# Attention's shift as one row, the closing norm on VectorE, and earlier work in the first stages of a one-core hybrid mixer

## The chip, the cores and the metric

The kernel runs on one NeuronCore of one Trainium2 chip. Its engines are TensorE (PE; PEld are its weight loads), VectorE (DVE), ScalarE (ACT), GpSimd (POOL) and SyncE (SP). SP issues nearly all DMA transfers. The metric is the device time of one execution in microseconds.

## The reference

x is 2048 rows of 1024 values. From a vector c come shift, scale and gate, each 1024 long, by `silu(c) @ w_ada + b_ada`. The layer then is:

```python
h = layer_norm(x) * (1 + scale) + shift
xr, zr, q, k, v, za, fl = split(h @ w_in)        # 512 wide each; fl is 8
xc = causal_conv4(xr)                             # per channel
y_r = rms_norm(rg_lru(xc)) * silu(zr)             # gated linear recurrence
d = cumsum(log_sigmoid(fl + b_fgate))             # per head
s = q @ k.T / 8 + (d[query] - d[key])             # 8 heads of 64, causal
y_a = rms_norm(softmax(s) @ v) * silu(za)
y = concat(y_r, y_a) @ w_out
out = layer_norm(2**0.25 * x + gate * y) * ln_gain + ln_bias
```

All is float32. A softmax row may be shifted by any number without changing its result.

## The kernel before

Products are made in float16 pairs: each operand is split into a high part and a low part (`split_out`, `split_T`, `split_h`), and three matmuls (high by high, high by low, low by high) add up in PSUM. Scales come from maxima over whole tensors. `all_max` takes a column of 128 partial maxima through a TensorE transpose, a VectorE maximum and a matmul with ones. Such chains are Python generators in the list `chains`; `tick` advances the first of them by one step, and `flush` runs all to their ends. A projection calls `tick` after every quarter or eighth of its matmuls.

The order of the program is a priority, not the order of the engines: a planner orders every engine's instructions with a timing model, and `issue_after(ins)` makes instructions stand behind `ins` on its engine. Pools of SBUF tiles with a fixed number of buffers (tags `r4` 8, `t2` 10, `wh` 7, `xr` 5, `H` 8) decide when a load may start.

The stages in order:

- Chunk 0 of x (512 rows; tiles `xt`). `load_x`, `norm_x`: statistics on VectorE, a power on POOL, scaling on ACT and POOL. For each of eight steps k, `scale_col` loads a slab of `w_ada` (`wadab`) and makes one column of the scale by eight one-column matmuls (`psc`), `load_w32` loads and splits 128 rows of `w_in` (`wrow`), `make_h32` transposes (`ptr`) and splits, and `xr32` does twelve matmuls (`pj<-h,w`).
- Chunk 1 the same way with the same weights. Beside it the shift is summed from slabs of `w_ada` (`wsh`, `pada`), column maxima of the weights are taken (`xam`, `xmax_fin`), four weight tiles are split (`wu`), chunk 2 is normalized, and `make_scale` finds the range of h.
- Chunks 2 and 3 with float16 pairs (`make_hk`, `xr_k`, evictions `hf`, `hT`); `finish_h` makes float16 pairs of chunks 0 and 1. In chunk 3 `vf_gen` splits the weights of v (`wN`, `wf`), and `xr_shift` makes four corrections (`pcj`, `cs`).
- Projections v, k, za, zr, q (`pj<-...`), with the recurrence (`lru_gen`) hooked in between, the decay sums (`decay_gen`), and the gate (`gate_gen`). Keys are stored to DRAM as `kd` (64 high rows, 64 low rows a head) and again in `kb` (64 high rows, two constant rows, two rows of the decay).
- Attention over 32 blocks (4 chunks of queries by 8 heads). `maxpass` runs ahead of each block: it loads `kk`, `qb`, `qs`, multiplies the high parts of queries and keys (`pmx`), takes row maxima (`mc`), turns them into a shift (`trow`) in two float16 rows (`Z`), and transposes these (`pzt`) into `qb`. `s_t` multiplies with the shift as extra contracted rows (`pst`), takes the exponential on ACT (`pf`), rounds it (`ph`) and subtracts for the low part, on POOL three times of four, on VectorE once. `av` multiplies with v (`acc`).
- Beside attention run the remaining q units, `wout_gen` (loads `woraw`, multiplies by the gate on POOL, splits), and `out_gen`: 16 output tiles of 128 rows, 48 matmuls each (`pout`), the residual (`xres`), `ln_gen` for the closing norm, and a store. `out_last` does the last tile's norm on VectorE. The last four output tiles follow the last block.

Of the kernel before, what the change touches and what calls it, by code (L numbers as in the profile page):

```python
# [19 lines left out]
P = 128  # L20
# [18 lines left out]
def hybrid_mixer(  # L39
# [66 lines left out]
    kb = dr.tile([H, 68, S], F16, name="kb", tag="kb")  # L106
# [27 lines left out]
    def load_cols(parts, name):  # L134
# [3 lines left out]
        for ap, k in parts:  # L138
            flat = ap[0] if len(ap.shape) == 2 else ap[0].rearrange("k n -> (k n)")
            nc.scalar.dma_start(rows[o:o + k, :], flat.rearrange("(a b) -> a b", b=P))  # L140
            o += k
# [6 lines left out]
    def all_max(col, n=1, gap=1):  # L148
# [45 lines left out]
    def pj_bank():  # L194
# [52 lines left out]
    def load_x(ci):  # L247
        xs = []
        for i in range(4):
# [5 lines left out]
            else:  # L255
                hv = [t2([P, CH], f"xt{g}") for g in range(2)]
                for g in range(2):
                    nc.sync.dma_start(hv[g], x[t * P:(t + 1) * P, g * CH:(g + 1) * CH])
# [70 lines left out]
    def make_scale():  # L329
# [7 lines left out]
        bda = yield from all_max(bd)  # L337
# [7 lines left out]
    def split_h(ci, k, hf):  # L345
        a = nc.scalar.copy(hT(k, 0, ci), hf).ins
        nc.vector.tensor_tensor(hT(k, 1, ci), hf, hT(k, 0, ci), ALU.subtract)  # L347
        return a
# [37 lines left out]
    def make_hk(ci, k, xs):  # L386
# [6 lines left out]
        hi_act[ci, k] = split_h(ci, k, hf)  # L393
# [236 lines left out]
    def scale_col(k):  # L630
# [33 lines left out]
    def wmax_fin():  # L664
        yield
        yield
        am = yield from all_max(wam, NW)
# [30 lines left out]
    def vf_gen(raws, fraw):  # L698
# [7 lines left out]
        am = yield from all_max(vf, 2)  # L706
# [3 lines left out]
        for q in range(4):  # L710
            w = wh([P, 2, 2, CH], "wN")
            nc.scalar.activation(w[:, 0], raws[q], AF.Copy, scale=rec[:, 0:1])
            nc.vector.scalar_tensor_tensor(w[:, 1], raws[q], rec[:, 0:1], w[:, 0], ALU.mult, ALU.subtract)
            wv.append(w)
        nc.scalar.activation(wf[:, :, 0:H], fraw, AF.Copy, scale=rec[:, 1:2])
        nc.vector.scalar_tensor_tensor(wf[:, :, H:2 * H], fraw, rec[:, 1:2], wf[:, :, 0:H], ALU.mult, ALU.subtract)
# [15 lines left out]

    pss = [bank(t, "pj") for t in "AAAO"]
    for k in range(KT + 2):
        if k < KT:
            scale_col(k)
            load_w32(k)
        if 0 < k <= KT:
            make_h32(0, k - 1, xs)
        if k == 4:  # L740
            xs1 = load_x(1)
        if 6 <= k < 6 + 4:
            norm_tile(xs1[k - 6], (1, 1, 1, 1,)[k - 6])
# [13 lines left out]
    def xmax_fin():  # L757
        xcol = sm([P, 4], "xcol")
        nc.vector.tensor_reduce(out=xcol, in_=xam, axis=AX.X, op=ALU.max)
        am = yield from all_max(xcol, 4)  # L760
        scales(am, RS, xinv, xrec)

    wu = []
    for k in range(KT + 2):
# [4 lines left out]
        if k < 4:  # L769
            for e in (2 * k, 2 * k + 1):  # L770
                with tc.issue_after(last["lo"]):
                    col_max(w32[e][:, 0].rearrange("p (j n) -> p j n", n=P), AX.X, xam[:, :, e])
        if k == 3:
            xs2 = load_x(2)
        if k == 4:
            chains.append(xmax_fin())
        if 2 <= k < 2 + 4:
            xraw.append(load_raw(P * len(xraw)))
        if k == 4:
            for g in range(2):  # L780
                nc.vector.tensor_tensor(va[g], va[g], pa[g], ALU.add)
        if k > 1:
            xr32(pss, 1, k - 2)
            tick()
        if k == 5:
# [833 lines left out]
```

## Time and profile before

| what | value |
|---|---|
| runs | 1213.55, 1217.73, 1219.83 us; median 1217.73 |
| profiled execution | 1211.64 us, span 1209.9 us |
| PE, DVE, ACT, POOL busy | 1111.2, 767.7, 719.6, 686.0 us |
| mean granted TensorE clock | 0.966 |

Busy time is the time in which an engine runs an instruction. A matmul counts as busy at whatever clock it is granted, so a slow clock lengthens busy time. "[2.31 <-ACT xt L266]" behind a row is the idle time just before it, and what ended it.

### The profile page before, as it was taken

How to read it: one execution, taken by the hardware profiler on the slowest of the kernel's cores; microseconds unless marked ns; L12 is line 12 of the kernel's file. 1: busy time of each engine (PE TensorE's matmuls, PEld its weight loads, DVE VectorE, ACT ScalarE, POOL GpSimd, SP SyncE). 2: the span in 40 equal slices, each digit the busy share in tenths (PEclk: the TensorE clock that was granted, in tenths of full speed). 3: DMA queues.
4: the chain of work that ended last, by engine and by line, in shares of the span. 5: the costliest groups of instructions: out<-in, count | busy, mean ns of one | idle time of the engine just before them, and what ended most of it. 6: DMA issues, size and time to landing. Idle time of an engine off the chain costs nothing. (4 is left out here: it accounts for less than half of the span.)

```text
span 1209.9 us, 20217 instructions
## 1 busy us (share of the span) xinstructions
PE 1111.2 (92%) x7467; PEld 622.8 (51%) x7467; DVE 767.7 (63%) x1435; ACT 719.6 (59%) x1244; POOL 686.0 (57%) x670
## 2 busy tenths in 40 slices
PE   6997899999999899999979979989999989999787
PEld 6874444454444444434445545555565555565444
DVE  4378775766668953664396544576677677667534
ACT  3437545564758412623375657577888688888841
POOL 5715532444554300830277645687788689887854
PEclk9998989999999999999979989989999999999899
DMA  9653046221225712754063344222332233221001
GB/s 296 208 151 123 1 118 189 71 64 33 70 70 141 242 55 70 260 160 140 26 205 114 95 129 123 87 93 86 101 94 90 76 103 106 78 89 46 18 27 70
DMA packets 110248, 130.56 MB, mean 108 GB/s; under 512 B 10086, under 2 KB 79318, under 8 KB 110150
## 3 DMA queue, kind: packets, MB, share of 16 engines
q1 hardware_dynamic: 109840, 129.17, 35.0%
q8 instruction: 58, 0.95, 0.3%
q14 instruction: 40, 0.33, 0.1%
q10 hardware_dynamic: 310, 0.12, 0.0%
HBM read 97.66 MB, written 31.59 MB: 107 GB/s over the span
## 5 line engine op out<-in xcount | busy, mean ns | idle before, releaser
L93 PE MATMUL pj<-hT,wT 128*128 128x512 f16 x1440 | 324.4, 383 | 4.1 <-DVE hT L347 1.7
L1294 POOL TENSOR_TENSOR ph<-pf,ph 128x512 f16<-128x512 f32 (+2 forms) x240 | 260.5, 1100 | 67.4 <-ACT ph L1292 62.6
L93 PEld LDWEIGHTS <-wT 128*128 128x128 f16 x1792 | 169.2, 99 | 208.6 <-issue 21.6
L1259 DVE TENSOR_REDUCE mc<-pmx 128x1 f32<-128x512 f32 (+2 forms) x320 | 184.8, 603 | 114.2 <-PE pmx L93 110.0
L1290 ACT ACTIVATE pf<-pst,bias 128x512 f32<-128x512 f32 (+1 forms) x320 | 194.7, 634 | 66.4 <-PE pst L93 58.8
L1292 ACT CAST ph<-pf 128x512 f16<-128x512 f32 (+1 forms) x320 | 171.7, 569 | 20.1 <-PE acc L93 15.9
L93 PE MATMUL acc<-V,ph 128*128 128x129 f16 (+1 forms) x2176 | 158.6, 210 | 22.0 <-POOL ph L1294 14.6
L93 PEld LDWEIGHTS <-ph 128*128 128x128 f16 x2176 | 124.1, 99 | 80.6 <-POOL ph L1294 22.1
L93 PE MATMUL pst<-qs,kk 128*128 128x512 f16 (+1 forms) x320 | 114.3, 360 | 2.0 <-DVE mc L1259 1.3
L93 PE MATMUL pst<-qb,kk 66*128 66x512 f16 (+1 forms) x320 | 112.8, 362 | 0.2
L93 PE MATMUL pmx<-kk,qb 68*128 68x512 f16 (+2 forms) x320 | 105.0, 357 | 7.4 <-DMA kk<-kb 3.8
L93 PE MATMUL pout<-wo,yT 128*128 128x512 f16 (+1 forms) x396 | 95.7, 372 | 1.5 <-ACT yT L1370 1.5
L93 PE MATMUL pout<-wo,yr 128*128 128x512 f16 (+1 forms) x396 | 94.1, 381 | 2.8 <-DVE zs L1369 2.7
L93 PE MATMUL pj<-wN,hT 128*128 128x512 f16 x384 | 89.5, 378 | 0.2 <-ACT XL L814 0.2
L1188 POOL TENSOR_TENSOR XL<-XL,szr 128x512 f32<-128x512 f32 x16 | 24.3, 1522 | 114.7 <-ACT szr L1185 114.7
L1296 DVE TENSOR_TENSOR ph<-pf,ph 128x512 f16<-128x512 f32 (+1 forms) x80 | 64.3, 804 | 33.8 <-ACT ph L1292 33.2
L93 PEld LDWEIGHTS <-kk 66*128 66x128 f16 (+1 forms) x640 | 55.1, 100 | 34.5 <-issue 11.6
L93 PE MATMUL pq<-hT,wT 128*128 128x512 f16 x288 | 67.0, 379 | 2.8 <-DVE qhl L881 2.8
L93 PEld LDWEIGHTS <-hT 128*128 128x128 f16 x640 | 44.5, 97 | 48.3 <-issue 3.6
L93 PEld LDWEIGHTS <-yr 128*128 128x128 f16 x396 | 38.3, 100 | 42.8 <-issue 8.0
L93 PEld LDWEIGHTS <-yT 128*128 128x128 f16 x396 | 37.5, 98 | 39.4 <-ACT yT L1370 1.7
L483 POOL TENSOR_TENSOR xl<-xc,xh 128x512 fp32r<-128x512 f32 x16 | 24.4, 1532 | 57.8 <-ACT xh L481 47.0
(307 smaller groups left out, 1846.0 us busy)
## 6 DMA issues: line engine op xcount, KB each, us to landing
wraw<-in_w_in_dram SPq DMA_DIRECT2D x40, 512.0 KB
woraw<-in_w_out_dram SPq DMA_DIRECT2D x16, 512.0 KB
xres<-in_x_dram SPq DMA_DIRECT2D x16, 512.0 KB
out_dram<-xres SPq DMA_DIRECT2D x15, 512.0 KB
wadab<-in_w_ada_dram SPq DMA_DIRECT2D x8, 512.0 KB
xt<-in_x_dram SPq DMA_DIRECT2D x16, 256.0 KB
xt<-in_x_dram SPq DMA_DIRECT2D x8, 512.0 KB
wsh<-in_w_ada_dram SPq DMA_DIRECT2D x16, 256.0 KB
```

Of the source, the lines that this page charges most:

```text
L93: m = nc.tensor.matmul(o, lhsT=l, rhs=r, start=st, stop=sp, skip_group_check=chk)
L483: nc.gpsimd.tensor_tensor(out=xl, in0=xc, in1=xh, op=ALU.subtract)
L1188: nc.gpsimd.tensor_tensor(out=XL[j][:, sl], in0=XL[j][:, sl], in1=sz, op=ALU.mult)
L1259: nc.vector.tensor_reduce(out=mc[:, i, b:b + 1], in_=ps[:, 0:w], axis=AX.X, op=ALU.max)
L1290: nc.scalar.activation(pf32[:, 0:w], ps[:, 0:w], AF.Exp, scale=DH ** -0.5, bias=bias[:, ci, h, kt:kt + 1])
L1292: nc.scalar.copy(ph[:, 0, 0:w], pf32[:, 0:w])
L1294: nc.gpsimd.tensor_tensor(out=ph[:, 1, 0:w], in0=pf32[:, 0:w], in1=ph[:, 0, 0:w], op=ALU.subtract)
L1296: nc.vector.tensor_tensor(ph[:, 1, 0:w], pf32[:, 0:w], ph[:, 0, 0:w], ALU.subtract)
```

## The change

The attention's shift becomes one float16 row: `Z` is written by one operation, one row is transposed, the matmuls contract 65 and 67 rows in place of 66 and 68, and `kb` keeps only three rows. The high key rows come from `kd` by a third load of `kk`, and the second store of the keys goes. The closing norm of the first 15 output tiles moves from ACT (one operation) and POOL (two) to VectorE (four half-width operations). In the first stages x is loaded first; idle matmuls (`spin`) run before and between the first steps; VectorE sums half of the slab for six of eight scale columns; vectors are loaded later on SP; normalizations, weight splits and column maxima are spread over steps and put behind evictions. Chains get more steps between their operations. POOL's 1024-wide gate operations are halved, and `woraw` is loaded two ahead.

```diff
-    kb = dr.tile([H, 68, S], F16, name="kb", tag="kb")
+    kb = dr.tile([H, 3, S], F16, name="kb", tag="kb")
...
-    def all_max(col, n=1, gap=1):
+    def all_max(col, n=1, gap=2):
+        yield
...
+    def spin(n):
+        for _ in range(n):
+            with tc.issue_after(last["pe"]) if "pe" in last else ExitStack():
+                mm(pw, warm[:, 0:P], warm, True, True)
+
+    spin(12)
+    ccol = load_cols([(c, 8), (b_ada, 24)], "ada", nc.scalar)
...
+    swarm = sm([P, 1], "swarm")
+    nc.scalar.activation(swarm, epsc, AF.Silu)
...
-        for q in range(KT):
+        NQ = KT if k < 2 else 4
+        sub = blk[:, KT - 1]
+        for q in range(NQ, KT):
+            if q == NQ:
+                nc.vector.tensor_scalar(sub, blk[:, KT - 1], cact[:, KT - 1:KT], None, ALU.mult)
+            else:
+                nc.vector.scalar_tensor_tensor(sub, blk[:, q - 1], cact[:, q - 1:q], sub, ALU.mult, ALU.add)
+        for q in range(NQ):
             mm(ps[:, 0:1], blk[:, q], cact[:, q:q + 1], q == 0, q == KT - 1, True)
+        if NQ < KT:
+            mm(ps[:, 0:1], sub, ones[:, 0:1], False, True, True)
...
-        am = yield from all_max(wam, NW)
+        am = yield from all_max(wam, NW, 6)
...
+            with tc.issue_after(last["hi"]), tc.issue_after(last["hlo"]):
+                nc.scalar.activation(w[:, 0], raws[q], AF.Copy, scale=rec[:, 0:1])
+                nc.vector.scalar_tensor_tensor(w[:, 1], raws[q], rec[:, 0:1], w[:, 0], ALU.mult, ALU.subtract)
             wv.append(w)
+            yield
...
+    spin(22)
+    for k in range(KT + 1):
         if k < KT:
+            with tc.issue_after(last["x0"]), tc.issue_after(last["pe"]):
+                scale_col(k)
+                load_w32(k)
+            with tc.issue_after(last["pe"]):
+                make_h32(0, k, xs)
+            if k < 2:
+                spin(4)
         if k == 4:
             xs1 = load_x(1)
+            vcol = load_cols([(conv_w, 16), (conv_b, 4), (b_gate_a, 4), (b_gate_x, 4), (lru_lambda, 4),
+                              (norm_lru, 4), (norm_attn, 4)], "vec", nc.sync)
...
+        if k > 0:
+            with tc.issue_after(last["pe"]):
+                xr32(pss, 0, k - 1)
+            with tc.issue_after(last["lo"]):
+                col_max(w32[k - 1][:, 0].rearrange("p (j n) -> p j n", n=P), AX.X, xam[:, :, k - 1])
...
+        if 3 <= k < 3 + 4:
+            with tc.issue_after(last["lo"]), tc.issue_after(hi_act[1, k]):
+                wu.append((split_T(xraw[k - 3], xrec[:, k - 3:k - 2]), xun[:, k - 3:k - 2]))
...
-            for j in range(4):
-                wu.append((split_T(xraw[j], xrec[:, j:j + 1]), xun[:, j:j + 1]))
-            norm_x(xs2, (1, 1, 1, 1,))
-            last["pow2"] = last["pow"]
+        if 4 <= k < 8:
+            norm_tile(xs2[k - 4], 1)
...
-        if k == 3:
-            cs = [xr_shift(j) for j in range(4)]
         tick()
+        if 3 <= k < 7:
+            cs.append(xr_shift(k - 3))
...
-            qk_store([(kd, 1, 0), (kb, None, 0)], p, hl, slice(half * D, (half + 1) * D))
+            qk_store([(kd, 1, 0)], p, hl, slice(half * D, (half + 1) * D))
...
-        nxt = wo_raw(0)
-        yield
+        raws = [wo_raw(0), wo_raw(1)]
+        yield
+        wo_gate(raws[0])
...
-        nc.sync.dma_start(kk[0:68, 1, 0:nk], kb[h, :, 0:nk])
+        nc.sync.dma_start(kk[0:DH, 1, 0:nk], kd[h, 0:DH, 0:nk])
+        nc.sync.dma_start(kk[DH:DH + 3, 1, 0:nk], kb[h, :, 0:nk])
...
-        t = sm([P, 4], "trow")
-        nc.vector.tensor_scalar(t, m, -1.0 / RS, ndc[:, ci, h:h + 1], ALU.mult, ALU.add)
-        nc.vector.tensor_copy(z[:, :, DH], t)
-        nc.vector.tensor_tensor(z[:, :, DH + 1], t, z[:, :, DH], ALU.subtract)
+        nc.vector.tensor_scalar(z[:, :, DH], m, -1.0 / RS, ndc[:, ci, h:h + 1], ALU.mult, ALU.add)
...
-        nc.scalar.activation(xt, xt, AF.Identity, scale=rs, bias=nm)
-        yield
-        nc.gpsimd.tensor_tensor(out=xt, in0=xt, in1=late["lng"], op=ALU.mult)
-        nc.gpsimd.tensor_tensor(out=xt, in0=xt, in1=late["lnb"], op=ALU.add)
+        for n in range(2):
+            ns = slice(n * CH, (n + 1) * CH)
+            nc.vector.scalar_tensor_tensor(xt[:, ns], xt[:, ns], mv[:, 0:1], late["lng"][:, ns], ALU.subtract, ALU.mult)
+            yield
+        for n in range(2):
+            ns = slice(n * CH, (n + 1) * CH)
+            nc.vector.scalar_tensor_tensor(xt[:, ns], xt[:, ns], rs, late["lnb"][:, ns], ALU.mult, ALU.add)
+            if n == 0:
+                yield
```

The gate weights (`load_gates`) and the constant row (`crow`) also move behind the last evictions of chunk 3, `xr_shift` uses another PSUM bank, and `decay_gen` and `gate_fin` wait one and two more steps.

More of the change, by code (lines that the diff above doesn't have):

```diff
@@ L346, in split_h @@
         a = nc.scalar.copy(hT(k, 0, ci), hf).ins
-        nc.vector.tensor_tensor(hT(k, 1, ci), hf, hT(k, 0, ci), ALU.subtract)
+        last["hlo"] = nc.vector.tensor_tensor(hT(k, 1, ci), hf, hT(k, 0, ci), ALU.subtract).ins
         return a
@@ L759, in xmax_fin @@
         nc.vector.tensor_reduce(out=xcol, in_=xam, axis=AX.X, op=ALU.max)
-        am = yield from all_max(xcol, 4)
+        am = yield from all_max(xcol, 4, 1)
         scales(am, RS, xinv, xrec)
     wu = []
+    chains.append(xmax_fin())
     for k in range(KT + 2):
@@ L769, in hybrid_mixer @@
         if k < 4:
-            for e in (2 * k, 2 * k + 1):
-                with tc.issue_after(last["lo"]):
-                    col_max(w32[e][:, 0].rearrange("p (j n) -> p j n", n=P), AX.X, xam[:, :, e])
+            xraw.append(load_raw(P * k))
         if k == 3:
             xs2 = load_x(2)
[L775 to L781, printed above, removed]
+            with tc.issue_after(last["lo"]):
+                for g in range(2):
+                    nc.vector.tensor_tensor(va[g], va[g], pa[g], ALU.add)
         if k > 1:
             xr32(pss, 1, k - 2)
-            tick()
-        if k == 5:
+        tick()
+        if 3 <= k < 3 + 4:
+            with tc.issue_after(last["lo"]), tc.issue_after(hi_act[1, k]):
+                wu.append((split_T(xraw[k - 3], xrec[:, k - 3:k - 2]), xun[:, k - 3:k - 2]))
+        if k == 4:
             flush()
@@ L855, in hybrid_mixer @@
     nc.scalar.dma_start(bfg, b_fgate[0].partition_broadcast(P))
-    load_gates()
+    with tc.issue_after(hi_act[3, KT - 1]), tc.issue_after(last["hlo"]):
+        load_gates()
     sp = sm([P, 4], "sp")
@@ L866, in hybrid_mixer @@
     crow = r4([2, S], "crow", F16)
-    nc.vector.memset(crow, RS)
-    nc.scalar.dma_start(kb[:, DH:DH + 2, :].rearrange("h a s -> a h s"), crow.unsqueeze(1).broadcast_to([2, H, S]))
-    QB = [cst([68, CH], f"qb{i}", F16) for i in range(4)]
+    with tc.issue_after(last["hlo"]):
+        nc.vector.memset(crow, RS)
+    nc.scalar.dma_start(kb[:, 0:1, :].rearrange("h a s -> a h s"), crow[0:1].unsqueeze(1).broadcast_to([1, H, S]))
+    QB = [cst([67, CH], f"qb{i}", F16) for i in range(4)]
     Z = [cst([P, 4, 68], f"Z{i}", F16) for i in range(4)]
     for q in QB:
-        nc.scalar.dma_start(q[66:68, :], crow[:, 0:CH])
+        nc.scalar.dma_start(q[65:67, :], crow[:, 0:CH])
     for z in Z:
@@ L1015, in wout_gen @@
                 split_out(w[:, 0, sl], w[:, 1, sl], raw[:, sl], so[:, k:k + 1])
+                if n == 0 and k + 2 < KT:
+                    raws.append(wo_raw(k + 2))
+                if n == 0 and k + 1 < KT:
+                    wo_gate(raws[0])
                 yield
@@ L1054, in v_fin @@
         yield
-        am = yield from all_max(col_max(vcolm))
+        col = col_max(vcolm)
+        yield
+        am = yield from all_max(col)
         inv = sm([P, 1], "vi")
@@ L1155, in a_fin @@
         yield
-        am = yield from all_max(col_max(zcol[:, TT:2 * TT]))
+        col = col_max(zcol[:, TT:2 * TT])
+        yield
+        am = yield from all_max(col)
         inv, rec = sm([P, 1], "ai"), sm([P, 1], "ar")
@@ L1255, in maxpass @@
                 end = b == ci
-                mm(ps[:, 0:w], qb[:, i * P:(i + 1) * P], kk[0:68, 1, b * CH:b * CH + w], True, not end)
+                mm(ps[:, 0:w], qb[:, i * P:(i + 1) * P], kk[0:67, 1, b * CH:b * CH + w], True, not end)
                 if end:
```

92 lines of the change are left out of this document (48 added, 44 removed).

## The prediction

> **What bounds the kernel now.** I read the page's head, then busy time by stretches cut where the order of work changes, then the timeline at the holes, the waits, and the groups by line.
>
> ```profile
> span 1209.9 us, 20217 instructions
> PE 1111.2 (92%) x7467; PEld 622.8 (51%) x7467; DVE 767.7 (63%) x1435; ACT 719.6 (59%) x1244; POOL 686.0 (57%) x670
> ```
>
> ```profile
> 0.00:34.40 34.40, 23.41 (x97) 21.57 (x98) 16.06 (x53) 12.44 (x18) 18.48 (x32) 1.00 0.97 299
> ...
> 94.40:105.90 11.50, 5.18 (x19) 3.56 (x20) 8.81 (x32) 7.01 (x13) 7.04 (x12) 0.71 0.51 190
> ...
> 144.40:161.80 17.40, 13.19 (x143) 8.59 (x140) 14.68 (x30) 10.44 (x16) 7.58 (x8) 0.61 0.49 127
> ...
> 408.00:421.00 13.00, 9.28 (x37) 4.21 (x35) 12.71 (x31) 1.37 (x2) 0.37 (x1) 0.87 0.88 292
> ...
> 518.00:527.00 9.00, 6.15 (x20) 2.21 (x19) 5.43 (x9) 0.41 (x1) 1.51 (x1) 0.81 0.59 178
> ...
> 600.00:720.00 120.00, 101.08 (x763) 58.43 (x761) 78.68 (x172) 79.66 (x169) 80.28 (x97) 0.90 0.46 138
> 720.00:860.00 140.00, 129.50 (x1029) 73.68 (x1028) 81.80 (x169) 95.34 (x190) 96.72 (x109) 0.95 0.32 98
> 860.00:1000.00 140.00, 132.24 (x1193) 78.40 (x1191) 104.97 (x196) 112.40 (x217) 111.26 (x118) 0.99 0.29 90
> 1000.00:1100.00 100.00, 99.19 (x885) 58.62 (x884) 70.44 (x128) 82.19 (x154) 85.97 (x82) 1.00 0.25 84
> 1100.00:1166.00 66.00, 54.46 (x509) 32.89 (x508) 34.14 (x60) 52.72 (x104) 51.59 (x51) 0.92 0.11 37
> ```
>
> The columns are stretch, length, busy time of PE, its weight loads, DVE, ACT and POOL, granted clock, DMA share, GB/s. PE is the bound: 1111 of 1210 us. What a change can win is PE's idle 99 us, plus the time PE works at a granted clock below 1, which follows each larger hole. From 1000 to 1100 nothing is to be had (99.19 of 100).
>
> **The start.** Work on x waits for x, which is issued behind weights.
>
> ```profile
> 2.33 9.20 SPq L258 DMA_DIRECT2D xt<-in_x_dram  x8
> ...
> 8.58 1.38 DVE L236 BATCH_NORM_STATS2 bst<-xt 128x6 f32<-128x512 f32 x2 [2.65 <-DMA xt<-in_x_dram]
> 8.70 1.28 ACT L206 ACT_TABLE_LOAD   x1 [8.70 <-DMA r_vec<-in_b_gate_x_dram]
> ...
> 18.50 0.16 DVE L244 SCALAR_TENSOR_TENSOR nm<-mv,rs 128x1 f32<-128x1 f32 x1 [0.60 <-POOL rs L242]
> ...
> 28.62 5.47 PE L93 MATMUL pj<-h,w 128*128 128x512 f32 x12
> ...
> 44.98 3.01 PE L93 MATMUL pj<-h,w 128*128 128x512 f32 x12
> 47.83 1.84 PE L93 MATMUL psc<-cact,wadab 128*128 128x1 f32 x16
> ...
> 49.92 3.01 PE L93 MATMUL pj<-h,w 128*128 128x512 f32 x12
> ...
> 58.06 3.02 PE L93 MATMUL pj<-h,w 128*128 128x512 f32 x12
> ...
> 64.12 0.60 PE L379 MATMUL ptr<-ident,xt 128*128 128x128 f32 x4
> ```
>
> Ahead of x stand one w_in row block and two scale slabs, by their shapes 1.3 MB, 4.2 us at the 299 GB/s of the first stretch. With x first, statistics begin at 8.6 - 4.2 = 4.4 us, and since four tiles took 8.58 to 18.66, the last scale is ready at 14.5. One normalization, transposes, an eviction pair and one more scale column stand between that and the first projection; I give them 6 us, so pj starts at 20.5 instead of 28.6. From there a step now has period 49.92 - 44.98 = 4.94 us. For six of eight columns VectorE takes half of the scale, 10 matmul records instead of 16: 6 x 1.84/16 = 0.69 us less, 4.25 us. In the kernel before the scale columns run ahead, and the last steps have none left (64.12 - 58.06 is two steps), so the stage's end is computed afresh: first projection, six steps, last projection, 20.5 + 2.9 + 6 x 4.25 + 2.9 = 51.8 against 64.1, 12.3 us. VectorE pays four 128x128 operations a column and a maximum, near 4 us of work per 4.25 us step as an estimate, which may cost part of it; POOL's split and join likewise. ACT's table now loads before its vector loads instead of after them (8.70); x is later than that, so it gains nothing by itself. The 42 spin matmuls lie before or between data that PE waits for (eight of them, 8 x 0.25 = 2 us at the later rate, do not and are in the 6 us). Seven vector loads move from ACT's queue to SP's, behind x's second chunk and ahead of the shift slabs: at most 1.15 us an issue by the xt row (9.20/8), 8 us of SP; the slabs behind them are needed only in the next stage's fourth step, by the times above some 25 us later: 0. I take **-10**; bounds 0 (VectorE or the slabs pace the stage) and -13.
>
> Here the clock column misleads: it says 1.00, but twelve pj took 5.47 us and later 3.01. The Trainium skill, TensorE: Matmul & The Clock Gate, Part 1, says the default is half rate and about 3.4 us of sustained work lifts it. By that rule spinning makes the first projection full rate; but this trace shows PE recorded busy 23.41 of 34.4 us, mostly with one-column matmuls, and still slow at 28.6. Without the spins' effect the start would give about 2.5 us less.
>
> **Second to third projection.** x's third chunk is normalized after four weight splits, so PE waits for it:
>
> ```profile
> 97.13 0.33 PE L390 MATMUL ptr<-ident,xt 128*128 128x128 f32 x1 [2.31 <-ACT xt L266]
> ```
>
> 11.5 us hold 5.18 of PE work, at clock 0.71. The change spreads the four normalizations and splits over steps 3 to 7 and finishes the column maxima a stage earlier. PE work at full rate would be about 3 us: bounds 0 and -8.5. I take **-8**, as DVE had free time in the stage before; late next would be the shift (Bcol).
>
> **Splits behind evictions.** V's splits stand ahead of the evictions PE needs:
>
> ```profile
> 147.60 3.23 ACT L712 ACTIVATE wN<-wraw,vfr 128x1024 f16<-128x1024 f32 x3 [5.53 <-DVE vfr L171]
> ...
> 151.79 1.97 PE L390 MATMUL ptr<-ident,xt 128*128 128x128 f32 x8 [2.54 <-ACT hf L392]
> ...
> 154.00 1.86 PE L93 MATMUL pj<-hT,wT 128*128 128x512 f16 x4 [0.24 <-ACT hT L346]
> ```
>
> The stretch 144.4 to 161.8 is 17.4 us for 13.19 us of PE work at clock 0.61, some 9 us at full rate. One split per step, behind the last eviction, and one shift column per step: bounds 0 and -8, taken **-6**. Late next: the fourth split, queued last, and the gate weights and the constant row, which now queue behind the last eviction; the V projection starts on other weights, and if that cover were gone the split would cost its 1.1 us (3.23/3).
>
> **More steps in chains.** PE met these before DVE was done:
>
> ```profile
> PE pam L151 <- DVE amc L166: 3.6, 2, 2.9
> ...
> PE pcs L93 <- DVE lfT L1092: 2.5, 1, 2.5
> ...
> PE pam L93 <- DVE amd L156: 2.0, 1, 2.0
> ```
>
> 8.1 us, and the two stretches 408:421 and 518:527 lose 0.13 x 13 and 0.19 x 9 of clock, 3.4 us. Chains get three steps longer where 16 ticks precede the next flush, so no flush pays. Bounds 0 and -11.5, taken **-7**: the sza wait in 408:421 stays.
>
> **Attention.** One row instead of two: the three DVE operations behind each maximum become one.
>
> ```profile
> PE acc L93 <- POOL ph L1294: 14.6, 20, 3.5
> PE pzt L93 <- DVE Z L1269: 9.1, 10, 2.3
> ```
>
> ```profile
> L1269 DVE TENSOR_TENSOR Z<-trow,Z 128x4 f16<-128x4 f32 x32 | 18.4, 574 | 0.9
> ...
> L1267 DVE TENSOR_SCALAR trow<-mrow,ndc 128x4 f32<-128x4 f32 x24 | 14.7, 614 | 0.7
> L1268 DVE CAST Z<-trow 128x4 f16<-128x4 f32 x32 | 14.5, 454 | 0.5
> ...
> L1427 DVE SCALAR_TENSOR_TENSOR xres<-xres,mv,lng 128x512 f32<-128x512 f32 x2 | 1.4, 746 | 0.0
> ```
>
> ```profile
> 839.46 2.35 POOL L1388 TENSOR_TENSOR xres<-xres,lnb 128x1024 f32<-128x1024 f32 x1
> ```
>
> ```profile
> 839.56 2.28 DVE L1269 TENSOR_TENSOR Z<-trow,Z 128x4 f16<-128x4 f32 x1
> ```
>
> ```profile
> 704.27 2.34 POOL L1003 TENSOR_TENSOR woraw<-woraw,gbc 128x1024 f32<-128x1024 f32 x1 [7.65 <-DMA woraw<-in_w_out_dram]
> ```
>
> ```profile
> L1385 ACT ACTIVATE xres<-xres,nm,rs 128x1024 f32<-128x1024 f32 x15 | 18.8, 1251 | 16.8 <-DVE nm L1384 16.7
> ```
>
> ```profile
> L1296 DVE TENSOR_TENSOR ph<-pf,ph 128x512 f16<-128x512 f32 x48 | 49.5, 1031 | 20.3 <-ACT ph L1292 20.0
> ```
>
> A four-element Z took 2.28 us and ended with POOL's norm operation: the two hold each other up. Removing 574 + 454 ns per block shortens the path to pzt by 1.03 us, 33 us of DVE over 32 blocks; of the 9.1 us of waits I expect 6 back. The closing norm takes 2 x 15 x 2.35 = 70 us off POOL and 18.8 off ACT, and puts 15 x 4 x 0.746 = 45 us on DVE, net 12 us more there. Its waits on POOL's ph (14.6) and the 7.65 us for which POOL stood before a weight still in flight (now loaded two ahead) shrink. POOL's halved 1024-wide operations block DVE half as long. In 600:1000 PE idles 120 - 101 + 140 - 130 + 140 - 132 = 37 us and loses 0.10 x 120 + 0.05 x 140 + 0.01 x 140 = 20 us of clock; in 1100:1166 11.5 and 5. Bounds: 0 and -45 (all waits named here with the clock behind them). I take **-14** and **-5**, under half, since PE next meets ACT's exp, which runs at 112 of 140 us. Fewer contracted rows (68 to 67, 66 to 65) change no streamed columns: 0. The key store to kb goes (16 issues), one more key load per block comes (32 issues), on SP; 16 more at 1.15 us is 18 us of queue time spread over 600 us and a block ahead: 0, and a few us if late. kb's smaller constant row: 0, since ACT only issues it.
>
> The Trainium skill, SBUF — State Buffer, SBUF: two separate sides, calls the pair shared by VectorE and GpSimd an exclusive lock: a VectorE operation with two SBUF inputs blocks GpSimd wholly and is blocked. The row of Z agrees. It speaks against the new norm: all 60 operations have two SBUF inputs. By it POOL would win 70 - 45 = 25 us, not 70; my -14 could survive on that.
>
> **Sum.** -10 - 8 - 6 - 7 - 14 - 5 = -50; for new waits I have not foreseen and DVE's added load +5: -45. The profiled execution took 1211.64 us (span 1209.9); the median of runs is 1217.73, 6.1 (0.5%) more, the lowest 1213.55. 1211.6 - 45 = 1166.6; half of the runs' surplus, 3, since a profile at the low end says little of the next median, gives **1170 us**.
>
> **Rivals.** (a) Only the front gains: attention stays paced by ACT and POOL's subtraction, -10 - 8 - 6 - 7 = -31, and the 5 back: 1185.6 + 3 = 1189. For: after 1100 ACT is busy 52.72 of 66. Against: the Z and norm rows. (b) The clock seldom falls: clock losses of the attention (25 us) go as well as half of them I counted: about 1148. For: they follow the holes. (c) New waits eat it. The chains' results come three steps later and each step is one projection quarter; if every one of the waits of 8.1 us and the holes of the front (8.5 + 8) merely moves to the user of the late result, what is left is the start's 10, and the 5 of new waits, doubled for the late results, take that: 1211.6 - 10 + 10 + 3 = 1215, no change. Against: the chains end ticks before the flush. (d) Slower: the norm on VectorE. A contended 512-wide VectorE operation averaged 1031 ns (ph row, against 0.746 for the similar uncontended one, 0.29 more). 60 of them are 62 us, standing in front of maxima and of ph's every fourth subtraction; if all reach PE, and they block POOL as long, attention loses 62 - 9 for the removed closing waits, 1211.6 - 31 + 53 + 3 = 1237. It decides once more than 45/60 = 0.75 us of each reaches PE. Against: DVE is busy only 82 to 105 of 140 us there.
>
> **Chances.** Forecast 0.55 (own range 1152 to 1182), (a) 0.22, (b) 0.10, (c) 0.06, (d) 0.07. Half a percent is about what a measurement of this kernel can tell. Faster 0.87, same 0.06, slower 0.07. The range 1140 to 1205 takes in (a) and (b).
>
> **What would show it.** First pj near 20 us and the stage's end near 52 to 55; no 2 us holes at the third chunk; pj after V's splits at 0.22 us each, not 0.43; PE's waits on Z under 3 us; POOL 70 us less busy, DVE some 10 more; granted clock above 0.98. I am wrong if PE waits at DMA-fed scale columns in the start, if DVE's maxima become what PE waits for, or if waits on ACT's exp replace those on POOL.

## The result and the profile after

The changed kernel takes 1148.81 us (median of four runs, 1147.51 to 1150.82), the kernel before 1216.48 us beside it: a ratio of 0.944, 95% interval 0.941 to 0.947, some 68 us. The forecast was 1170, with a range of 1140 to 1205. The direction held, and so did that range, which was drawn to take in two rivals. The forecast's own range, 1152 to 1182, did not hold: the time came out 21 us below the forecast, and one term of the sum holds most of that.

The head of the page after, the profiled execution of 1150.82 us:

```profile
span 1149.1 us, 20239 instructions
PE 1091.7 (95%) x7473; PEld 611.2 (53%) x7473; DVE 787.0 (68%) x1441; ACT 707.1 (62%) x1234; POOL 627.7 (55%) x655
```

Up to the last matmul, PE's idle time falls from 91.7 to 50.4 us, 41 us of the 61 us by which the span shrank. The time recorded at half clock falls from 85 to 54 us; half of the difference, 16 us, is most of the rest. The clock records leave out the start: they begin at 34.4 us before, although the first projections ahead of that still took 5.47 us instead of 3.01, and at 4.7 us after.

Busy time by stage, before and then after, with the columns of the prediction (stretch, length, PE, PEld, DVE, ACT, POOL, clock, DMA share, GB/s). The cuts are the same places of the work: chunk 0; chunk 1 up to the first projection of chunk 2; chunk 3; v; and from the fifth row on the attention's four chunks.

```profile
0.00:64.50 64.50, 52.24 (x267) 46.47 (x267) 27.78 (x72) 27.40 (x42) 42.74 (x53) 1.00 0.83 256
64.50:105.90 41.40, 33.17 (x161) 25.73 (x160) 31.53 (x74) 17.95 (x27) 8.29 (x13) 0.92 0.51 166
...
132.60:169.40 36.80, 32.33 (x264) 18.08 (x263) 27.37 (x48) 18.26 (x29) 18.98 (x19) 0.81 0.34 89
169.40:272.90 103.50, 101.48 (x624) 51.53 (x624) 66.67 (x88) 56.04 (x80) 35.31 (x29) 1.00 0.35 99
...
591.00:665.00 74.00, 63.23 (x498) 37.93 (x496) 54.55 (x125) 50.15 (x108) 51.15 (x64) 0.91 0.46 139
665.00:801.20 136.20, 120.82 (x957) 68.91 (x956) 75.49 (x159) 90.64 (x182) 86.17 (x102) 0.96 0.37 110
801.20:965.70 164.50, 156.61 (x1324) 91.11 (x1322) 112.92 (x213) 121.67 (x237) 124.91 (x131) 0.95 0.28 88
965.70:1157.40 191.70, 177.99 (x1638) 106.16 (x1636) 129.83 (x232) 160.73 (x306) 163.17 (x158) 0.97 0.22 71
```

```profile
0.00:58.90 58.90, 53.58 (x273) 40.70 (x273) 42.07 (x104) 26.92 (x42) 39.49 (x51) 0.91 0.87 266
58.90:96.60 37.70, 31.81 (x161) 25.20 (x159) 28.23 (x60) 17.46 (x27) 11.36 (x15) 0.95 0.63 198
...
122.50:149.80 27.30, 27.02 (x259) 15.34 (x258) 18.53 (x35) 18.03 (x29) 20.73 (x16) 1.00 0.01 1
149.80:256.50 106.70, 102.46 (x624) 51.46 (x624) 79.63 (x117) 63.79 (x88) 39.97 (x34) 1.00 0.46 129
...
566.10:636.00 69.90, 64.21 (x484) 38.28 (x482) 48.66 (x107) 48.82 (x106) 55.94 (x70) 0.88 0.49 151
636.00:750.50 114.50, 111.07 (x927) 64.80 (x926) 71.36 (x141) 86.81 (x179) 78.18 (x97) 0.99 0.40 120
750.50:899.70 149.20, 144.34 (x1318) 87.01 (x1316) 111.53 (x213) 118.26 (x235) 108.87 (x123) 1.00 0.34 103
899.70:1096.70 197.00, 185.87 (x1687) 111.17 (x1685) 139.16 (x241) 156.77 (x302) 140.26 (x150) 0.97 0.22 70
```

The first score matmul comes 25 us earlier (566.1 against 591.0), and the attention takes 530.6 instead of 566.3 us, 36 less. Most of the latter stands in chunk 1 (136.2 to 114.5) and chunk 2; chunk 3 is longer, because work came to it: it holds 265 output matmuls (`pout`) instead of 217, chunk 1 only 87 instead of 120.

It is tempting to read this as "the front's edits gave 25 us, the attention's edits 36". The experiments show that this reading is wrong.

The waits after, of the lines that the prediction named:

```profile
DVE mc L1315 <- PE pmx L93: 84.1, 73, 4.9
...
PE acc L93 <- POOL ph L1347: 4.4, 8, 1.3
...
PE pzt L93 <- DVE Z L1322: 0.3, 1, 0.3
```

The last two were 14.6 and 9.1 us before. The first is time that VectorE has to spare.

### The profile page after: what moved, and what is told of

It is laid out like the page before. It is cut to its first block, busy times and chain, and to the rows that moved or that the text cites. A ratio compares the mean times of both kernels' runs of the same rounds, so it can differ in the third digit from the quotient of the medians.

```text
span 1149.1 us, 20239 instructions
## 1 busy us (share of the span) xinstructions
PE 1091.7 (95%) x7473; PEld 611.2 (53%) x7473; DVE 787.0 (68%) x1441; ACT 707.1 (62%) x1234; POOL 627.7 (55%) x655
## 4 chain that ended last, share of the span: by engine, by line
PE 65%; DVE 11%; ACT 8%; issue 6%; POOL 5%; DMA 4%; SPq 0%; DVEq 0%; ACTq 0%; POOLq 0%
PE pj L93 25%; PE pout L93 12%; PE pst L93 8%; PE pq L93 6%; PE acc L93 5%; PE pmx L93 4%; DVE mc L1315 2%; POOL ph L1347 1%; PE pgate L93 1%; ACT pf L1343 1%; DVE xres L1442 1%; DMA zs<-zd 1%; POOL XL L636 1%; ACT ph L1345 1%; DVE wadab L648 1%
## 5 line engine op out<-in xcount | busy, mean ns | idle before, releaser
L93 PE MATMUL pj<-hT,wT 128*128 128x512 f16 x1440 | 321.1, 381 | 2.6 <-DVE sza L1192 2.6
L1347 POOL TENSOR_TENSOR ph<-pf,ph 128x512 f16<-128x512 f32 (+2 forms) x240 | 263.8, 1111 | 108.5 <-ACT ph L1345 92.6
L93 PEld LDWEIGHTS <-ph 128*128 128x128 f16 x2176 | 126.5, 99 | 67.8 <-POOL ph L1347 8.8
L93 PE MATMUL pst<-qs,kk 128*128 128x512 f16 (+1 forms) x320 | 111.6, 351 | 4.1 <-DVE mc L1315 2.9
L93 PE MATMUL pst<-qb,kk 65*128 65x512 f16 (+1 forms) x320 | 110.5, 354 | 0.9 <-ACT qb L1330 0.8
L93 PE MATMUL pmx<-kk,qb 67*128 67x512 f16 (+2 forms) x320 | 104.1, 353 | 4.5 <-DVE mc L1315 2.7
L93 PE MATMUL pout<-wo,yr 128*128 128x512 f16 (+1 forms) x396 | 91.5, 373 | 1.5 <-DVE zs L1422 1.5
L1349 DVE TENSOR_TENSOR ph<-pf,ph 128x512 f16<-128x512 f32 (+1 forms) x80 | 54.8, 685 | 24.0 <-ACT ph L1345 23.2
L93 PEld LDWEIGHTS <-kk 65*128 65x128 f16 (+1 forms) x640 | 53.8, 99 | 29.2 <-issue 8.2
```

The costliest lines, as they stand in the source:

```text
L93: m = nc.tensor.matmul(o, lhsT=l, rhs=r, start=st, stop=sp, skip_group_check=chk)
L1347: nc.gpsimd.tensor_tensor(out=ph[:, 1, 0:w], in0=pf32[:, 0:w], in1=ph[:, 0, 0:w], op=ALU.subtract)
L1349: nc.vector.tensor_tensor(ph[:, 1, 0:w], pf32[:, 0:w], ph[:, 0, 0:w], ALU.subtract)
```

## The experiments

Each kernel was timed beside the kernel before, whose median moved between 1213.3 and 1221.7 us from one set to the next. So ratios compare the kernels, not microseconds of different rows; 0.001 is 1.2 us, and differences under about 0.005 are not told apart. Losses given below in us are differences of ratios, unless they are of profiled executions. The last four columns are of the profiled executions, by matmul records: first score matmul, the attention's length (to the last `acc`), PE's idle time in it, and chunk 1 of it.

| kernel | median us | ratio | 95% interval | first score | attention | idle in it | chunk 1 |
|---|---|---|---|---|---|---|---|
| before | 1216.48 | 1 | | 591.0 | 566.3 | 47.8 | 136.2 |
| after | 1148.81 | 0.944 | 0.941 to 0.947 | 566.1 | 530.6 | 25.1 | 114.5 |
| attention's edits alone | 1200.45 | 0.986 | 0.982 to 0.989 | 592.5 | 554.0 | 40.9 | 133.9 |
| front alone, keys as before | 1167.24 | 0.959 | 0.953 to 0.964 | 567.0 | 548.3 | 38.4 | 114.8 |
| front alone, keys as after | 1165.21 | 0.960 | 0.956 to 0.964 | 565.0 | 544.5 | 34.9 | 113.1 |
| norm back, 1024 wide | 1161.20 | 0.956 | 0.951 to 0.961 | 563.3 | 544.1 | 37.0 | 117.4 |
| norm back, 512 wide | 1155.03 | 0.951 | 0.947 to 0.955 | 565.1 | 535.9 | 28.9 | 114.4 |
| two shift rows | 1157.36 | 0.953 | 0.949 to 0.957 | 564.8 | 537.7 | 33.0 | 114.7 |
| all chains short | 1172.10 | 0.963 | 0.959 to 0.967 | 574.0 | 540.7 | 32.5 | 131.0 |
| the attention's two chains short | 1161.62 | 0.953 | 0.948 to 0.957 | 564.9 | 542.5 | 35.3 | 131.6 |
| splits not ordered | 1153.78 | 0.946 | 0.941 to 0.951 | 567.0 | 531.9 | 27.6 | 113.5 |
| no spins | 1155.03 | 0.948 | 0.944 to 0.953 | 567.6 | 533.7 | 27.2 | 114.3 |
| scale all on TensorE | 1149.77 | 0.943 | 0.939 to 0.948 | 562.4 | 532.6 | 29.6 | 113.6 |
| x maxima a step later | 1160.07 | 0.950 | 0.944 to 0.955 | 567.0 | 540.2 | 30.0 | 117.1 |

### Front and attention apart

The front alone: the norm, the shift rows and the output weights as in the kernel before.

```diff
-        raws = [wo_raw(0), wo_raw(1)]
...
+        nxt = wo_raw(0)
...
-        nc.vector.tensor_scalar(z[:, :, DH], m, -1.0 / RS, ndc[:, ci, h:h + 1], ALU.mult, ALU.add)
+        t = sm([P, 4], "trow")
+        nc.vector.tensor_scalar(t, m, -1.0 / RS, ndc[:, ci, h:h + 1], ALU.mult, ALU.add)
+        nc.vector.tensor_copy(z[:, :, DH], t)
+        nc.vector.tensor_tensor(z[:, :, DH + 1], t, z[:, :, DH], ALU.subtract)
...
-            nc.vector.scalar_tensor_tensor(xt[:, ns], xt[:, ns], mv[:, 0:1], late["lng"][:, ns], ALU.subtract, ALU.mult)
...
+        nc.scalar.activation(xt, xt, AF.Identity, scale=rs, bias=nm)
+        yield
+        nc.gpsimd.tensor_tensor(out=xt, in0=xt, in1=late["lng"], op=ALU.mult)
+        nc.gpsimd.tensor_tensor(out=xt, in0=xt, in1=late["lnb"], op=ALU.add)
```

> The changed kernel with all three attention edits undone: norm on ScalarE and GpSimd, two shift rows, output weights loaded one ahead and multiplied 1024 wide. If the parts before the attention stand by themselves as the two profiles have them (first score matmul 24.9 us earlier), this is about 1217 - 25 = 1192 us (1185 to 1197), and the three edits together are worth about 40 us. If the earlier front is what fills the attention better (work that was due later is done by then), it is nearer to the changed kernel, 1150 to 1170 us.

It came to 0.960: the second expectation. With these three edits undone, the attention was still 22 us shorter than before, and again most of it in chunk 1. Two more kernels followed. One undid the layout and loads of the keys as well (`kb` with 68 rows); the other is the complement, the kernel before with the attention's edits alone.

> All of the attention as it was before, the layout and the loads of the key rows included (68 rows in one store and one load); the front alone is new. The run that undid the norm, the single row and the output weights' prefetch, but kept the new layout of the keys, came to 1165.2 us (ratio 0.960), and its attention was still 22 us shorter than before. Theory L (the layout is what gave those 22 us): 1180 to 1190 us, chunk 1 of the attention back above 130 us. Theory F (the front's earlier finish leaves the attention in a better order, whatever its code): 1160 to 1169 us, chunk 1 near 113 us.

> The kernel before with the attention's edits alone (closing norm on VectorE, one shift row with its key layout, output weights two ahead and multiplied in halves); the front is old. If the attention's edits carry the 36 us by which its stages shrank: 1177 to 1184 us. If they carry only what undoing them in the changed kernel gave back (16 us) and the rest comes with the front: 1197 to 1203 us.

0.959 and 0.986. The layout of the keys makes no difference that can be told; the attention's edits alone are worth 17 us (ratio 0.982 to 0.989), the front's alone 50, and together they make up the 68 of the whole change. The profiled attention shrinks by 12 us with its own edits (566.3 to 554.0). So a large part of what the attention's stages gained is the work of edits that the prediction counted with the front.

### The chains

```diff
-    def all_max(col, n=1, gap=2):
-        yield
+    def all_max(col, n=1, gap=1):
...
-        am = yield from all_max(wam, NW, 6)
+        am = yield from all_max(wam, NW)
```

> The changed kernel with its chains of maxima as short as before (one step between, no extra step at the start, the weights' chain one step). The prediction put 7 us on the chains (bounds 0 and 11.5). By it 1154 to 1160 us, with PE gaps of 1 to 3 us back ahead of the transposes of the column maxima (pam) at four to six places. If other work covers these places now: 1147 to 1151 us.

0.963, 23 us slower: more than either theory, and more than the bound of 11.5 in the prediction. (This undoes two of the steps that each chain got; a third, a `yield` between a column maximum and `all_max`, stays.) The profiled executions differ by 19 us. 8 us of it lie ahead of the first score matmul, where the waits on chain results are back (the profile's waits of this run):

```profile
PE pam L151 <- DVE amc L166: 5.4, 2, 4.1
PE pam L93 <- DVE amd L156: 3.3, 1, 3.3
```

10 us lie in the attention, where chunk 1 is again 131 us with 120 output matmuls. Only two chains run there: the maxima of the fourth z group and of the output weights. The next kernel shortens these two and leaves the others (the condition is true from the attention on):

```diff
     def all_max(col, n=1, gap=2):
-        yield
+        if psum["same"]:
+            gap = 1
+        else:
+            yield
```

> The changed kernel with only the two chains that run during the attention (the maxima of the fourth z group and of the output weights) as short as before; all chains ahead of the attention keep their extra steps. With all chains short the run was 23 us slower (ratio 0.963 against 0.944), 8 us of it ahead of the first score matmul and 10 behind it. Theory S (a step more in a chain of the attention's side work moves all filler behind it, so that less of the output projection is spent in chunk 1 and more is left for chunk 3): 1157 to 1163 us, chunk 1 again with 120 output matmuls instead of 87 and above 128 us. Theory F (the front's chains do it, by starting the attention earlier): 1148 to 1152 us, chunk 1 near 114 us.

0.953, 1161.6 us: theory S. Two steps in each of two chains are worth 10 us, while the first score matmul comes no later than in the changed kernel (564.9 against 566.1). Its chunk 1 and chunk 3, and what PE and SP waited for in chunk 1:

```profile
637.50:769.00 131.50, 121.50 (x978) 69.52 (x977) 76.49 (x152) 90.78 (x185) 83.36 (x104) 0.96 0.38 111
...
916.20:1107.40 191.20, 178.42 (x1644) 107.52 (x1642) 135.94 (x234) 153.24 (x299) 136.16 (x145) 0.97 0.24 72
```

```profile
PE pmx L93 <- DMA kk<-kd: 5.8, 1, 5.8
```

```profile
SPq L1299 <- POOL woraw L1052: 5.6, 1, 5.6
```

The timeline at that place, in order of time:

```profile
653.83 0.46 SPq L1302 DMA_DIRECT2D qb<-qd  x1
...
657.43 2.48 POOL L1052 TENSOR_TENSOR woraw<-woraw,gbc 128x512 f32<-128x512 f32 x2 [0.19 <-DMA woraw<-in_w_out_dram]
...
659.94 0.33 SPq L1299 DMA_DIRECT2D kk<-kd  x1
...
663.58 0.59 PE L93 MATMUL pmx<-kk,qb 67*128 67x512 f16 x1 [5.82 <-DMA kk<-kd]
```

SP stood until POOL had multiplied a tile of the output weights, then loaded the keys of the next block, and PE had waited 5.8 us for them; half clock begins in this hole and lasts from 660.5 to 670.7. In chunks 0 and 1 `kk` is taken from the same ring of eight buffers (`r4`) as `woraw`; in the later chunks it is not. The kernel with the attention's edits alone shows the same hole in its chunk 1:

```profile
690.25 0.58 PE L93 MATMUL pmx<-kk,qb 67*128 67x512 f16 x1 [5.54 <-DMA kk<-kd]
```

The kernel before waits 3.8 us for `kk` in its chunk 1, in three pieces. Behind the `woraw` operation at 704.27 that the prediction quotes, PE waits 3.53 us, but there for POOL's `ph`, which follows that operation on POOL.

With longer chains the multiplications of the output weights begin at 595 us instead of 580 and end at 670 instead of 660, so they fall elsewhere between the loads of `kk`. In the changed kernel one load of `kk` still waits for POOL, but for a shorter time, and PE waits for no `kk` in chunk 1:

```profile
SPq L1296 <- POOL woraw L1049: 3.4, 1, 3.4
```

The shift of 33 output matmuls itself is no gain; they are paid mostly in chunk 3, which takes 197.0 us in the changed kernel against 191.2. In the attention the run with two short chains has 10.2 us more idle PE time than the changed kernel and 3.4 us more at half clock, 1.7 lost: together the 11.9 by which its attention is longer. The hole is 5.8 of the 10.2. Other waits of PE are longer too, in the changed kernel 4.4 us for POOL's `ph` and 0.3 for Z, and with the two chains short:

```profile
PE acc L93 <- POOL ph L1350: 8.8, 17, 1.7
PE pzt L93 <- DVE Z L1325: 4.6, 6, 1.9
```

Why these grew, which of the two chains does it, and whether the ring's order does it alone, was not tried.

So of the attention's 36 us, 12 came with its own edits (566.3 to 554.0) and 12 with two steps in each of two chains (542.5 to 530.6). The 12 between them (554.0 to 542.5) came with other parts of the front. The runs below that undo single parts of the front (splits, spins, scale) leave the attention within some 3 us of the changed kernel, so which part it is stays open. These thirds are rough: one profile of the same attention code took 540 us instead of 531.

### The norm and the shift row

> The changed kernel with its closing norm put back as it was: one ScalarE operation and two 1024-wide GpSimd operations per output tile. The changed kernel stands at 1148.8 us, and its attention is 36 us shorter than before. Theory A (the wide GpSimd operations block VectorE, and GpSimd's own 70 us of norm delay the split operand ph): most of the 36 us comes back, 1170 to 1180 us, PE's waits for ph return from 4 to more than 10 us, and GpSimd is 65 to 70 us busier. Theory B (the norm's place does not matter, the attention gained by the single shift row): 1147 to 1153 us. Theory C (the norm on VectorE costs something there): below 1146 us.

0.956: 14 us slower than the changed kernel, its attention 13.5 longer. The norm's place matters in the direction of theory A, but less than theory A put on it, and PE's waits for POOL's `ph` only rose from 4.4 to 7.4 us. GpSimd is 59 us busier (686.8). What rose more are PE's waits for Z, from 0.3 us, although the shift is one row here too:

```profile
PE pzt L93 <- DVE Z L1322: 5.7, 4, 2.7
```

```diff
         for n in range(2):
             ns = slice(n * CH, (n + 1) * CH)
...
+            nc.gpsimd.tensor_tensor(out=xt[:, ns], in0=xt[:, ns], in1=late["lng"][:, ns], op=ALU.mult)
+            nc.gpsimd.tensor_tensor(out=xt[:, ns], in0=xt[:, ns], in1=late["lnb"][:, ns], op=ALU.add)
```

> As the one before, but GpSimd's four operations of a tile are 512 wide instead of two of 1024. GpSimd's busy time is about the same, the longest single operation is half as long (about 1.2 instead of 2.3 us). If long operations that VectorE must stand behind are what costs, this is nearer to the changed kernel than the run with 1024-wide ones, by half of that run's loss or more; if it is the amount of GpSimd's work, the two agree within 3 us.

The same work on GpSimd in halves ran beside it at 1153.8 to 1156.5 against 1158.5 to 1162.4 us: 6 us better, nearly half of the loss, with GpSimd as busy (689.0). So part of the price is how long one operation holds the other engine up. The groups of VectorE's own `ph` show it, in the changed kernel, with the norm back 1024 wide, and with it 512 wide:

```profile
L1349 DVE TENSOR_TENSOR ph<-pf,ph 128x512 f16<-128x512 f32 x48 | 40.8, 850 | 16.0 <-ACT ph L1345 15.9
```

```profile
L1349 DVE TENSOR_TENSOR ph<-pf,ph 128x512 f16<-128x512 f32 x48 | 52.7, 1098 | 21.0 <-ACT ph L1345 20.8
```

```profile
L1349 DVE TENSOR_TENSOR ph<-pf,ph 128x512 f16<-128x512 f32 x48 | 46.2, 963 | 24.3 <-ACT ph L1345 20.2 <-POOL ph L1347 3.8
```

The same operation takes 850, 1098 and 963 ns. PE's waits for Z show it too: with the norm 512 wide none is left. The other half of the loss looks like GpSimd's load: what stays longer with the norm 512 wide is PE's wait for POOL's `ph`, 8.4 us against 4.4, and PE's idle time in the attention is 3.8 us longer in all. That is read from one profile each, not tried.

```profile
PE acc L93 <- POOL ph L1347: 8.4, 10, 1.4
```

> The changed kernel with the attention's shift put back into two rows: three VectorE operations instead of one per head and chunk, 66 instead of 65 rows in the score matmuls and the transposes; norm stays on VectorE. Theory B (single row is the gain): 1165 to 1180 us, PE's waits for Z back to several us. Theory A (norm's place is the gain): 1149 to 1155 us, 64 pairs of small VectorE operations of 0.2 to 0.3 us each added, about 30 us of VectorE, next to none on the path.

0.953, 10 us slower than the changed kernel, between the two expectations; PE's waits for Z are 8.0 us (0.3 after). (The edit adds 64 small VectorE operations, not 64 pairs, and 18 us of VectorE, not 30.) So neither the single row alone (5.7 us with the norm 1024 wide on GpSimd) nor the norm's move alone removed the waits for Z. Norm and row undone singly cost 14 and 10 us, all three edits of the attention together 19: they partly cover the same holes. The output weights' prefetch was not run alone.

### The front's parts

```diff
-            with tc.issue_after(last["hi"]), tc.issue_after(last["hlo"]):
-                nc.scalar.activation(w[:, 0], raws[q], AF.Copy, scale=rec[:, 0:1])
+            nc.scalar.activation(w[:, 0], raws[q], AF.Copy, scale=rec[:, 0:1])
...
+        if k == 3:
+            cs = [xr_shift(j) for j in range(4)]
         tick()
-        if 3 <= k < 7:
-            cs.append(xr_shift(k - 3))
...
-    with tc.issue_after(hi_act[3, KT - 1]), tc.issue_after(last["hlo"]):
-        load_gates()
+    load_gates()
...
-    with tc.issue_after(last["hlo"]):
-        nc.vector.memset(crow, RS)
+    nc.vector.memset(crow, RS)
```

> The changed kernel with the splits of V's weights issued all at once and with no order behind the evictions, the four shift columns in one place, the gates' weights and the fill of the constant row with no order. The prediction put 6 us on this (bounds 0 and 8); the stage of the third chunk became 9.5 us shorter. By the prediction: 1153 to 1157 us; by the whole stage: 1158 to 1160 us, PE holes of 1 to 2 us and half clock back between 119 and 155 us; if the longer chains alone emptied these holes: 1148 to 1151 us.

0.946, not told from 0.944. Its 1153.8 us lie in the first expectation, but only because the kernel before was slower in that set too (1221.7 us). The stages show why so little is lost. Chunk 3 and the v projection are:

```profile
120.20:154.90 34.70, 30.18 (x259) 16.09 (x258) 28.33 (x49) 19.04 (x31) 22.79 (x20) 0.85 0.36 93
154.90:256.30 101.40, 101.39 (x623) 51.53 (x623) 66.90 (x88) 56.01 (x80) 36.96 (x30) 1.00 0.35 102
```

The hole at V's splits is back (3.3 us and 10.2 us at half clock), and chunk 3 takes 34.7 instead of 27.3 us; but v takes 101.4 instead of 106.7 us with no idle PE. In the changed kernel v has this wait, which it lacks here:

```profile
PE pgate L93 <- ACT xh L489: 3.9, 3, 1.6
```

Of 7.4 us, 5.3 are given back in the very next stage, where the matmuls of the recurrence's gates (`pgate`) wait for their rounded input `xh`. Why `xh` comes late there was not tried.

No spins (`mm` once instead of 42 times):

> The changed kernel with one idle matmul at the start instead of 42. By the clock theory (only full matmuls lift the granted clock, the one-column matmuls of the scale do not) the half rate lasts until a few us after the first projections, some 30 us from the start: first projections near 21 to 24 us as now, but their first 7 us at 0.38 instead of 0.24 us a matmul, so 3 to 6 us in all: 1152 to 1155 us. If the spins' clock is worth nothing (loads bound the start): 1147 to 1150 us. If the spins themselves stand in the way of the scale's matmuls: below 1146 us.

0.948, with an interval that reaches the changed kernel's. The number fits the first expectation, the place does not: the chunk 0 stage ends at the same time with and without spins (58.9 us both), and so does the way to the first projection of chunk 2 (96.6 and 96.7). So the 4.5 us between the two do not lie where the spins are, and are not explained. PE's timeline with spins, then without:

```profile
1.54 6.89 PE L93 MATMUL pw<-warm 128*128 128x512 f16 x24 [1.54 <-DVE warm L200]
...
13.45 2.20 PE L93 MATMUL psc<-cact,wadab 128*128 128x1 f32 x16 [2.58 <-DMA wadab<-in_w_ada_dram]
...
17.89 3.41 PE L93 MATMUL psc<-cact,wadab 128*128 128x1 f32 x16
...
23.62 3.83 PE L93 MATMUL pj<-h,w 128*128 128x512 f32 x12
...
28.71 2.98 PE L93 MATMUL pj<-h,w 128*128 128x512 f32 x12
```

```profile
12.37 3.54 PE L93 MATMUL psc<-cact,wadab 128*128 128x1 f32 x16 [5.89 <-DMA wadab<-in_w_ada_dram]
...
21.69 4.37 PE L93 MATMUL pj<-h,w 128*128 128x512 f32 x12 [0.66 <-ACT h L389]
...
27.32 3.01 PE L93 MATMUL pj<-h,w 128*128 128x512 f32 x12
```

The clock that the spins had raised (records of full clock from 4.7 us) fell at 14.9 and came back at 25.2, within the first projection, whose twelve matmuls took 3.83 us instead of 2.98. PE was recorded busy all that time (changed kernel, busy time by stretches):

```profile
14.90:25.20 10.30, 10.30 (x40) 8.13 (x40) 5.53 (x14) 5.56 (x9) 6.81 (x7) 0.50 1.11 347
```

Without spins full clock is first recorded at 24.6.

The change of one line, `NQ = KT`, puts the whole scale back on TensorE (24 one-column matmuls more, 4 in each of 6 columns, and 6 fewer that added VectorE's part):

> The changed kernel with all eight products of a scale column on TensorE, as before, for all eight columns. Per column 4 one-column matmuls of about 0.2 us go back to TensorE (8 x 6 x 4 / 8 = 24 matmuls, some 5 us of TensorE) and 24 VectorE operations go. If TensorE paces the first stage: first stage 3 to 5 us longer, 1152 to 1154 us. If the loads pace it (DMA share 0.87 there): 1147 to 1150 us, the first stage within 1 us of 58.9.

0.943, no difference, as in the second expectation; its stage lies between the two. Chunk 0 took 60.4 us with PE busy 56.8, against 58.9 with 53.6: 1.5 us of the 4.1 that the prediction counted for the shorter steps.

Last, the attempt at a better version: the chain of the x projection's maxima appended at k == 1 instead of before the loop.

> The changed kernel with the chain of the x projection's maxima started one step later, behind the first transposes of the second chunk's loop instead of ahead of it. It stands at a gap of TensorE of 3.13 us (waiting for the column maxima) with 3.4 us at half clock behind it. If that wait goes, 3 to 5 us less: 1144 to 1146 us, and the second chunk's stage is 28 to 30 us instead of 32.5. If the wait only moves to the scale's result, which the weight splits of the next steps need: 1147 to 1151 us.

0.950, runs at 1150, 1159, 1161 and 1162 us: outside both expectations, though the interval reaches the changed kernel's. The stage is not shorter (32.1 against 32.5 us, a gap of 2.7 us now ahead of a transpose). The loss of the profiled run is in the attention, whose code is that of the changed kernel: 540.2 against 530.6 us. The gap of 3.13 us was also a weak thing to build on. Kernels with the same lines there show 0.2 us (norm back, 1024 wide, with 1.2 more behind it), 1.9 (512 wide) and 2.3 (no spins) ahead of that transpose. Nothing run here is told to be faster than the changed kernel.

## Why the prediction was right, and where its sizes were off

- **Attention, -14 and -5, with +5 for new waits: right in size.** Its edits alone gave 17 us, which also answers rival (a), only the front gains. The named waits went: PE's for Z to 0.3 us (under 3 forecast), for `ph` to 4.4. POOL lost 58 us of work, not 70, since some of its other operations grew. DVE gained 19, not 10: the norm takes 58.5 us of it instead of 45, and the scale sums of the first stage 14 that this figure left out, while `ph` takes 9 less. The norm's two groups after:

```profile
L1442 DVE SCALAR_TENSOR_TENSOR xres<-xres,rs,lnb 128x512 f32<-128x512 f32 x30 | 32.1, 1099 | 1.0 <-POOL rs L1451 0.9
L1438 DVE SCALAR_TENSOR_TENSOR xres<-xres,mv,lng 128x512 f32<-128x512 f32 x30 | 26.4, 921 | 0.0
```

- **Rival (d)** had this price nearly right: 0.35 and 0.18 us above the 0.746 us of the uncontended operation, where it assumed 0.29. But little of it reaches PE, whose waits for the maxima `mc` are 5.6 us after and 3.6 before. VectorE stands 84 us waiting for `pmx`, so it has the time. By the Trainium skill, SBUF — State Buffer, SBUF: two separate sides, such an operation and a GpSimd operation that reads SBUF block each other. The rows show both halves. VectorE's durations follow the length of GpSimd's operations. GpSimd's 512-wide `ph` was not lengthened (1193 ns here, 1203 before and 1208 with the norm back), but its power `rs` of one element a partition was, which here stands beside the norm's operations on VectorE. All 16 of them end 0.40 to 0.42 us after a two-input VectorE operation ends. In the kernel before (603 ns; 606 with the norm back, 1024 wide), then in the changed kernel:

```profile
L1395 POOL TENSOR_TENSOR rs<-ve,mhalf 128x1 f32<-128x1 f32 x16 | 9.7, 603 | 11.7 <-DVE ve L1393 11.7
```

```profile
L1451 POOL TENSOR_TENSOR rs<-ve,mhalf 128x1 f32<-128x1 f32 x16 | 15.5, 969 | 25.5 <-DVE ve L1449 23.4 <-PE acc L93 1.3 <-PE pout L93 0.7
```

- **Chains, -7, bounds 0 and -11.5: the step that failed.** They are worth 23 us. The prediction priced them by the waits on chain results that the trace shows ahead of the attention; there 8 us came, near the forecast. It did not see that two chains run in the attention's list of side work, where a step counts as a turn, and moves loads and the POOL work that holds a ring of buffers: 10 us. The 16 us missed here are most of the 21 by which the forecast was high. The wait of 5.8 us for `kk` is traced to the ring; how the rest comes about stays open.
- **Splits, -6: right in the stage, wrong in the sum.** The holes went (27.0 of 27.3 us busy, clock 1.00), 9.5 us in the stage; v gave 3.2 back, and undoing it changes the whole by less than can be told. The prediction named the gate weights as late next, and priced that at nothing; what PE waits for there is the gates' input.
- **Start, -10: half of it came.** The stage is 5.6 us shorter, ending at 58.9 instead of 52 to 55. Statistics begin at 5.1 us and the last scale of x is ready at 15.1, close to the 4.4 and 14.5 of the prediction; but from there the first projection took 8.5 us instead of the 6 given, and stands at 23.6. (It lies between 20.3 and 23.7 in the profiles with spins.) The first scale column waited for its load (2.58 us), one of the prediction's own signs of being wrong, and the spins did not give the first projection full clock. The steps after it were to shrink from 4.94 to 4.25 us. Some did (28.71 to 32.95), but the first took 5.1, and one took 6.25 with a wait of 0.96 us for VectorE's part of a scale column. The x maxima, finished a stage earlier, cost chunk 1 a gap of 3.1 us in this profile, and 0 to 2.3 us in others. Loading x first was not run alone.
- **Second to third projection, -8: 6.4** (11.7 to 5.2 us between the last projection of chunk 1 and the first of chunk 2).
- **Rival (b)**, the clock, gave 1148, the right number by luck: recorded clock is 16 of the 61 us, and in the attention about 10 of the 25 us that the rival counted on (51 to 30 us at half clock). The mean granted clock is 0.977, not above 0.98.
- **The sum** is closer than its terms: the chains came out 16 us larger than counted, while start, splits and the second to third projection came out smaller.

## What to carry to other kernels

Where side work is dealt out in turns, a turn more in one chain moves every later load and buffer release: price an edit there by what it shifts, and run it alone. A stage's gain is no measure of the edits made in that stage; two complementary kernels, each with one half of the change, showed here that only 12 of the attention's 36 us came with its own edits, and a third kernel that 12 belonged to two chains. And of a wait that is removed, follow the late part into the next stage: the splits won 7.4 us in one stage and lost 5.3 in the next.

## What the runs showed of the hardware

- That PE is recorded busy was not enough here to raise the granted clock. With mostly one-column matmuls, some transposes and eight spins it stayed at half for 10.3 us of unbroken work; without spins, one-column matmuls and transposes from 12.37 on did not bring full clock, which was first recorded at 24.6, 2.9 us after the projections began at 21.69. The Trainium skill, TensorE: Matmul & The Clock Gate, Part 1, has about 3.4 us of sustained work raise it. With the first spins (from 1.54, full at 4.7 us: 3.2) and with the projections the trace agrees; for this mix of one-column matmuls and transposes it does not. Which of the two does not count was not tried.
- The same VectorE operation took 850 ns on average with the norm on VectorE, 963 with it on GpSimd in halves, and 1098 with it there 1024 wide. The other way round, a GpSimd operation of one element a partition took 969 instead of 603 ns beside the norm's operations on VectorE.
- The identical attention program took 531 to 534 us in four profiles and 540 in a fifth whose only edit lies 500 us earlier. That one recorded 41 us at half clock in the stretches that began in the attention, the others 27 to 34.
